# Second mixer: block masks and token scales by ScalarE, the block diagonal issued three steps ahead of its transposes, one tile of sums for a head's chunks

## The chip, the cores and the metric

The kernel runs on one core of one Trainium2 chip. The metric is the device time of one execution in microseconds, the lower the better. TensorE (PE in the profile) multiplies matrices, VectorE (DVE), ScalarE (ACT) and GpSimd (POOL) work elementwise, and SyncE (SP) issues the transfers (DMA). Each engine works through its own list of instructions strictly in the order of the list; an instruction whose input is not there yet holds up everything behind it on that engine.

## The reference, cut to what matters

The whole model is long (two attention layers, then two layers with feed-forward parts, a mixer and cross attention each, for 512 tokens of width 1024). The change touches one mixer alone, the gated delta rule of the second layer, with 8 heads of width 128:

```python
def deltanet_mixer(h, w_in, conv_w, a_log, dt_bias, o_norm, w_out):
    qkv, z, a, b = jnp.split(h @ w_in, ...)
    qkv = jax.nn.silu(causal_dwconv(qkv, conv_w)).astype(jnp.float32)
    q, k, v = jnp.split(qkv, 3, axis=-1)
    q, k, v = l2norm(q.reshape(shp)), l2norm(k.reshape(shp)), v.reshape(shp)
    ...
    o = gated_delta_rule_chunked(q, k, v, g, beta)
    o = rmsnorm(o, o_norm) * jax.nn.silu(z...)
    return o.reshape(B, S, W) @ w_out

def gated_delta_rule_chunked(q, k, v, g, beta):
    ...
    decay = jnp.exp(jnp.where(tril, gcum[..., :, None] - gcum[..., None, :], -jnp.inf))
    kkt = jnp.einsum('bhnid,bhnjd->bhnij', kb, k) * decay
    amat = jnp.eye(C) + jnp.where(strict, kkt, 0.0)
    sol = lax.linalg.triangular_solve(amat, rhs, left_side=True, lower=True, unit_diagonal=True)
    ...
    def step(state, inp):
        v_new = u_i - jnp.einsum('bhcd,bhde->bhce', w_i, state)
        o = (jnp.einsum('bhcd,bhde->bhce', q_i * jnp.exp(g_i)[..., None], state)
             + jnp.einsum('bhij,bhje->bhie', qk_i, v_new))
        state = (state * ... + jnp.einsum('bhcd,bhce->bhde', k_i * ..., v_new))
        return state, o
```

The kernel works with 4 chunks of 128 tokens, so that a head has four 128x128 triangular matrices to invert.

## The kernel before, in words

The mixer (`mixer1`) runs in ten stages, s = 0 to 9. In stage s three generators are woven together: `head(s)` projects and convolves k, q, z and v of head s, makes the decays e and the strictly triangular matrix U; `inverse` inverts the triangular matrices of head s-1; `steps` walks through the four chunks of head s-2 with the running state. Some 41 us pass for each stage. The order on TensorE is the order in which this weave yields; the orders on the other engines are set by a scheduler with priorities and estimated costs, which here can put an instruction far ahead of the place where the code issues it.

The inversion goes in levels. `solve` writes the 16x16 diagonal blocks of U to DRAM, reads them back so that each lies in one partition, and inverts them there on GpSimd with 30 small instructions (L1653 and L1655, T and Y); the result Y goes to DRAM (yd, L1659) and comes back as soC, 128 partitions x 4 x 16 numbers (L1661). `inverse` first spreads soC into the block diagonal X (128x512, four chunks of 128) by one product with a mask of zeros and ones (L1674), transposes it on TensorE (L1683), and then doubles the block size by two levels, with the off-diagonal blocks B, the product of U and another mask (L1692), as input.

Other names: rk, the inverse lengths of the keys, scale e by one product on GpSimd in `key` (L1591). `steps` multiplies the head's output o by the inverse lengths rq, also on GpSimd (L1770), ahead of the transposes of o (L1775). In `steps` the products with the state are po<-state,kT and po<-state,qT (L1732, L1733); R (DVE, L1735) and oq (ACT, L1738) read them; po<-R,X (L1740) gives vn (ACT, L1742); po<-vn,A and po<-vn,kd give o and the new state on DVE. Each chunk takes a new tile of PSUM with the tag "po", of which there is one buffer.

Around them ACT splits weights: wh is the rounded weight (ACT, L114), wl the rest (DVE, L115), from the loaded ws. In the convolution of k, q or v, xp is the padded projection, xc the sum of four shifted copies (one on ACT, L1292, three on DVE, L1296), and kT, qT, vT the result (tanh on ACT, L1536; product on DVE, L1537). kT and vT are transposed on TensorE (L1550) into kd and vb (DVE, L1628, L1629). sq<-kT (ACT, L1578) feeds the lengths (PE, L1580).

Of the kernel before, what the change touches and what calls it, by code (L numbers as in the profile page):

```python
# [8 lines left out]
F32 = mybir.dt.float32  # L9
F32R = mybir.dt.float32r  # L10
I32 = mybir.dt.int32
AF = mybir.ActivationFunctionType
OP = mybir.AluOpType
AX = mybir.AxisListType

P = 128
D = 1024
NCH = 8
S = 512
# [1141 lines left out]
class Block2:  # L1161
# [323 lines left out]
    def decays(self, pool):  # L1485

        net, nc, I = self.net, self.net.nc, self.net.I
        out = {}
        yield from self.proj(I["dn_ab"], out, "p1", 16)
        yield  # L1490
        ab = pool.tile([P, S], F32, name="ab", tag="dnB", bufs=1)[:16, :]
        nc.vector.tensor_tensor(ab, out["ps"], self.rb[:16, :], op=OP.mult)
        pt = net.psum("p3")
        for t in range(4):
            nc.tensor.transpose(pt[:, t * 16:(t + 1) * 16], ab[:, t * P:(t + 1) * P], net.ident[:16, :16])
        t3 = lambda name: pool.tile([P, 4, 8], F32, name=name, tag=f"dc{name}", bufs=1)
        v = pt[:, :64].rearrange("p (t a) -> p t a", a=16)
        dt = net.bcast_row(I["dn_dt_bias_2"][0], 8, "dtb", pool)
        al = net.bcast_row(I["dn_a_log_2"][0], 8, "alog", pool)
        beta, x, gc = t3("beta"), t3("x"), t3("gc")  # L1500
        nc.scalar.activation(beta, v[:, :, 8:16], AF.Tanh, scale=0.5)
        nc.vector.tensor_scalar(beta, beta, 0.5, 0.5, op0=OP.mult, op1=OP.add)
        nc.vector.tensor_tensor(x, v[:, :, 0:8], dt.unsqueeze(1).to_broadcast([P, 4, 8]), op=OP.add)
        sp = self.softplus(x.rearrange("p t h -> p (t h)"), 32, pool)
        nc.scalar.activation(al, al, AF.Exp)
        nc.vector.scalar_tensor_tensor(x, sp.rearrange("p (t h) -> p t h", h=8), -1.0,
                                       al.unsqueeze(1).to_broadcast([P, 4, 8]), op0=OP.mult, op1=OP.mult)
        yield
        pg = net.psum("p3")
        g2 = x.rearrange("p t h -> p (t h)")  # L1510
        nc.tensor.matmul(pg[:, 0:32], net.c["triu"], g2, start=True, stop=True)
        nc.tensor.matmul(pg[:, 32:64], net.c["ones"], g2, start=True, stop=True)
        nc.vector.tensor_copy(gc, pg[:, 0:32].rearrange("p (t h) -> p t h", h=8))
        gl = pg[:, 32:64].rearrange("p (t h) -> p t h", h=8)
        ngc, egc, egl, dk = t3("ngc"), t3("egc"), t3("egl"), t3("dk")
        nc.vector.tensor_scalar(ngc, gc, -1.0, None, op0=OP.mult)
        nc.scalar.activation(egc, gc, AF.Exp)
        nc.scalar.activation(egl, gl, AF.Exp)
        nc.vector.tensor_tensor(dk, gl, gc, op=OP.subtract)
        nc.scalar.activation(dk, dk, AF.Exp)  # L1520
        self.dc = dict(beta=beta, gc=gc, ngc=ngc, egc=egc, egl=egl, dk=dk)
        yield
# [16 lines left out]
    def head(self, h, hd, pool, late):  # L1539

        net, nc, I = self.net, self.net.nc, self.net.I
        cw = self.cw
        q4 = lambda a: a.rearrange("p (t d) -> p t d", d=P)
        bc = lambda a: a.unsqueeze(2).to_broadcast([P, 4, P])
        tl = lambda name, bufs: pool.tile([P, S], F32, name=name, tag=f"dn{name}", bufs=bufs)
# [6 lines left out]
        cols = lambda a: lambda t: a[:, t * P:(t + 1) * P]  # L1552
# [9 lines left out]
        dc, e, U, A = {}, tl("e", 1), tl("U", 2), tl("A", 3)  # L1562
# [21 lines left out]
        def key():  # L1584
            rk = st["k"]
            for n in ("b", "s", "w"):
                st[n] = small("n" + n)
            nc.vector.tensor_tensor(st["b"], rk, dc["beta"], op=OP.mult)
            nc.vector.tensor_tensor(st["s"], rk, dc["dk"], op=OP.mult)
            nc.vector.scalar_tensor_tensor(st["w"], st["b"], -1.0, dc["egc"], op0=OP.mult, op1=OP.mult)  # L1590
            nc.gpsimd.tensor_tensor(out=q4(e), in0=q4(e), in1=bc(rk), op=OP.mult)  # L1591

        def product(m, n):
            ps = net.psum("p3")
# [69 lines left out]
    def inverse(self, hd, pool, wait):  # L1664

        net, nc = self.net, self.net.nc
        mm = nc.tensor.matmul
        q4 = lambda a: a.rearrange("p (t d) -> p t d", d=P)
        tl = lambda name, bufs: pool.tile([P, S], F32, name=name, tag=f"dn{name}", bufs=bufs)
        lev = lambda l: self.lev[:, (l - 4) * P:(l - 3) * P].unsqueeze(1).to_broadcast([P, 4, P])  # L1670
        U = hd["U"]
        hd["X"] = X = tl("X", 2)
        blocks = [P, 4, 8, 16]
        nc.gpsimd.tensor_tensor(out=X.rearrange("p (t m b) -> p t m b", t=4, b=16),  # L1674
                                in0=hd["blocks"].unsqueeze(2).to_broadcast(blocks),
                                in1=self.lev[:, 2 * P:].rearrange("p (m b) -> p m b", b=16).unsqueeze(1).to_broadcast(blocks),
                                op=OP.mult)
        Z = tl("Z", 1)
        for _ in range(wait):
            yield  # L1680
        ps = net.psum("pT")
        for t in range(4):
            nc.tensor.transpose(ps[:, t * P:(t + 1) * P], X[:, t * P:(t + 1) * P], net.ident)  # L1683
        nc.scalar.activation(Z, ps, AF.Copy)
        tiles = [slice(t * P, (t + 1) * P) for t in range(4)]
        for l in range(4, 6):
            n = 1 << l
            half = lambda a, i: a.rearrange("p (m two b) -> p m two b", two=2, b=n)[:, :, i, :]
            dense = lambda a: a.rearrange("p (m b) -> p m b", b=n)
            B, W = tl("B", 1), tl("W", 2)  # L1690
            nc.gpsimd.memset(W, 0.0)
            nc.gpsimd.tensor_tensor(out=q4(B), in0=q4(U), in1=lev(l), op=OP.mult)  # L1692
            yield
            pw = net.psum("pT")
            for t, sl in enumerate(tiles):
                mm(dense(pw[:, t * 64:(t + 1) * 64]), B[:, sl], half(Z[:, sl], 0), start=True, stop=True)
            nc.scalar.activation(half(W, 0), dense(pw[:, :256]), AF.Copy)
            yield
            px = net.psum("p1")
            for t, sl in enumerate(tiles):  # L1700
                mm(dense(px[:, t * 64:(t + 1) * 64]), W[:, sl], half(X[:, sl], 1), start=True, stop=True)
                mm(dense(px[:, 256 + t * 64:256 + (t + 1) * 64]), X[:, sl], half(W[:, sl], 0), start=True, stop=True)
            nc.vector.tensor_tensor(half(X, 1), half(X, 1), dense(px[:, :256]), op=OP.subtract)
            nc.vector.tensor_tensor(half(Z, 0), half(Z, 0), dense(px[:, 256:]), op=OP.subtract)
        yield
        h0, h1 = slice(0, HD), slice(HD, P)
        right = lambda a, t: a[:, t * P + HD:(t + 1) * P]
        pw = net.psum("pT")
        for t in range(4):
            mm(pw[h1, t * HD:(t + 1) * HD], right(U, t)[h0], Z[h0, t * P:t * P + HD], start=True, stop=True)  # L1710
        W = tl("W", 2)
        nc.scalar.activation(W[h1, :256], pw[h1, :256], AF.Copy)
        yield
        px = net.psum("p1")
        for t in range(4):
            mm(px[h0, t * HD:(t + 1) * HD], W[h1, t * HD:(t + 1) * HD], right(X, t)[h1], start=True, stop=True)
        nc.vector.tensor_scalar(q4(X)[h0, :, HD:], px[h0, :256].rearrange("p (t d) -> p t d", d=HD), -1.0, None, op0=OP.mult)

    def steps(self, h, hd, pool):

        net, nc = self.net, self.net.nc
        mm = nc.tensor.matmul
        small = lambda name, bufs=2: pool.tile([P, P], F32, name=name, tag=f"st{name}", bufs=bufs)
        q4 = lambda a: a.rearrange("p (t d) -> p t d", d=P)
        o = pool.tile([P, S], F32, name="o", tag="dno", bufs=2)
        state = None
        for t in range(4):
            sl = slice(t * P, (t + 1) * P)
            ps = net.psum("po")
            R = hd["vb"][:, sl]  # L1730
            if t:
                mm(ps[:, 0:P], hd["kT"][:, sl], state, start=True, stop=True)  # L1732
# [12 lines left out]
            if t < 3:  # L1745
# [7 lines left out]
                state = new  # L1753
# [10 lines left out]
        rq = net.small([P, 4], "orq")  # L1764
# [2 lines left out]
        nc.vector.tensor_tensor(ss, ss, rq, op=OP.mult)  # L1767
        r = net.rsqrt(ss, 4, 1.0 / P, EPS)
        nc.vector.tensor_tensor(rq, r, rq, op=OP.mult)
        nc.gpsimd.tensor_tensor(out=q4(o), in0=q4(o), in1=rq.unsqueeze(2).to_broadcast([P, 4, P]), op=OP.mult)  # L1770

        def finish():
            ps = net.psum("p3")
# [7 lines left out]
    def mixer1(self):  # L1781
        net, nc, I = self.net, self.net.nc, self.net.I
        stats = self.norm("mix_norm_2", 1)
        with net.tc.tile_pool(name="mix1", bufs=2) as pool:
            self.lev = pool.tile([P, 3 * P], F32, name="lev", tag="lev", bufs=1)
            nc.sync.dma_start(self.lev, I["lev"])
            self.cw = pool.tile([P, 96], F32, name="cwh", tag="cwh", bufs=1)
            nc.vector.tensor_scalar(self.cw, net.col["dn_conv_w_2"], 0.5, None, op0=OP.mult)
            hds = [{} for _ in range(8)]
# [373 lines left out]
```

## Time and profile before

| what | value |
|---|---|
| median of 3 runs | 3684.03 us (3679.31 to 3688.05) |
| profiled execution | 3685.61 us, span 3682.5 us |
| PE busy over the span | 3589.7 us, 97% |
| DVE, ACT, POOL busy | 57%, 37%, 19% |
| granted TensorE clock, mean | 0.993 of full speed |

The mixer of the change takes some 400 us of the span, from about 2780 to 3195 us. The profiled execution is one single execution, 1.6 us above the median; all durations below are from it.

### The profile page before, as it was taken

The numbers are of one execution on the slowest core, as the hardware profiler recorded it, in microseconds if no ns is written. First come the engines' busy times: TensorE is split into PE (matmuls) and PEld (weight loads), VectorE is DVE, ScalarE is ACT, GpSimd is POOL, SyncE is SP. The second block draws the span as 40 slices with busy tenths as digits, with TensorE's granted clock in tenths as the row PEclk, the third lists the DMA queues.
The fourth block names the chain that finished last, engine by engine and source line by source line (L and its number), as shares of the span: only waits on it lengthen the run. The fifth ranks groups of instructions, "written<-read, shape, count | busy, mean of one in ns | idle before, by whom it ended". The sixth has DMA issues, their size and how long they took to land.

```text
span 3682.5 us, 51253 instructions
## 1 busy us (share of the span) xinstructions
PE 3589.7 (97%) x19626; PEld 2992.9 (81%) x19626; DVE 2096.6 (57%) x4095; ACT 1380.4 (37%) x2413; POOL 715.7 (19%) x889
## 2 busy tenths in 40 slices
PE   8999999999999999999999999999999999999998
PEld 6888778888877778888778888888888887788887
DVE  6655765875566553335666433443347887664335
ACT  4334543244345332224644322322243333443223
POOL 1123330003233010101420100110013444101001
PEclk9999999999999999999999999999999999999999
DMA  8322115533212533333122333333333212323333
GB/s 278 101 73 63 49 54 192 160 123 97 83 62 68 194 103 96 96 92 107 54 98 69 98 97 98 97 92 103 97 98 112 57 56 74 116 78 92 102 96 106
DMA packets 137012, 366.68 MB, mean 100 GB/s; under 512 B 30144, under 2 KB 43712, under 8 KB 136256
## 3 DMA queue, kind: packets, MB, share of 16 engines
q1 hardware_dynamic: 136768, 363.42, 31.7%
q8 instruction: 154, 2.52, 0.3%
q14 instruction: 90, 0.74, 0.1%
HBM read 332.82 MB, written 20.84 MB: 96 GB/s over the span
## 4 chain that ended last, share of the span: by engine, by line
PE 85%; DVE 7%; DMA 3%; ACT 2%; issue 1%; POOL 1%; SPq 0%; DVEq 0%; ACTq 0%; POOLq 0%
PE p L131 14%; PE p L133 14%; PE p L132 14%; PE pS L131 7%; PE pS L132 6%; PE pS L133 6%; PE po L562 2%; PE po L131 2%; PE po L133 2%; PE po L132 2%; DVE wl L115 2%; PE pT L132 2%; PE pT L131 2%; PE pT L133 2%; PE pS L536 1%
## 5 line engine op out<-in xcount | busy, mean ns | idle before, releaser
L114 ACT ACTIVATE wh<-ws 128x1024 fp32r<-128x1024 f32 (+4 forms) x561 | 563.3, 1006 | 1395.4 <-PE p L132 673.3
L115 DVE TENSOR_TENSOR wl<-ws,wh 128x1024 fp32r<-128x1024 f32 (+4 forms) x561 | 659.2, 1176 | 224.4 <-ACT wh L114 222.4
L131 PE MATMUL p<-nh,wh 128*128 128x512 f32 x1084 | 430.1, 397 | 4.5 <-ACT nh L1179 2.0
L133 PE MATMUL p<-nh,wl 128*128 128x512 f32 x1084 | 424.0, 391 | 4.0 <-DVE wl L115 4.0
L132 PE MATMUL p<-nl,wh 128*128 128x512 f32 x1084 | 423.9, 391 | 1.9 <-DVE nl L115 1.9
L1246 POOL TENSOR_TENSOR g<-g,rb 128x512 f32<-128x512 f32 x88 | 150.2, 1709 | 1138.3 <-ACT g L1245 1138.3
L131 PE MATMUL pS<-nh,wh 128*128 128x512 f32 x620 | 255.1, 411 | 1.0 <-DVE xr L1229 1.0
L133 PEld LDWEIGHTS p<-nh,wl 128*128 128x128 f32 x1084 | 203.3, 188 | 49.4 <-DVE wl L115 5.5
L133 PE MATMUL pS<-nh,wl 128*128 128x512 f32 x620 | 243.4, 393 | 0.0
L132 PE MATMUL pS<-nl,wh 128*128 128x512 f32 x620 | 242.7, 391 | 0.0
L131 PEld LDWEIGHTS p<-nh,wh 128*128 128x128 f32 x1084 | 203.5, 188 | 47.0 <-ACT nh L1179 2.4
L132 PEld LDWEIGHTS p<-nl,wh 128*128 128x128 f32 x1084 | 203.7, 188 | 42.1 <-DVE nl L115 2.2
L1244 DVE TENSOR_TENSOR g<-p,rb 128x512 f32<-128x512 f32 x88 | 60.4, 691 | 226.5 <-PE p L133 213.4
L131 PE MATMUL p<-hxh,wh 128*128 128x512 f32 (+1 forms) x480 | 187.3, 390 | 0.8 <-DVE wT L545 0.8
L132 PE MATMUL p<-hl,wh 128*128 128x512 f32 (+1 forms) x488 | 179.8, 369 | 0.0
L133 PE MATMUL p<-hh,wl 128*128 128x512 f32 (+1 forms) x488 | 179.4, 368 | 0.0
L131 PE MATMUL p<-hh,wh 128*128 128x512 f32 (+1 forms) x488 | 179.3, 368 | 0.0
L133 PE MATMUL p<-hxh,wl 128*128 128x512 f32 (+1 forms) x480 | 173.5, 361 | 0.0
L132 PE MATMUL p<-hxl,wh 128*128 128x512 f32 (+1 forms) x480 | 172.9, 360 | 0.0
L1188 POOL TENSOR_TENSOR acc<-acc,sq 128x512 f32<-128x512 f32 x48 | 73.9, 1539 | 483.2 <-ACT sq L1187 482.8
L552 POOL TENSOR_SCALAR p<-p,rinv 128x768 f32<-128x768 f32 (+2 forms) x128 | 104.4, 816 | 254.5 <-DVE rinv L551 138.4
L1259 DVE SCALAR_TENSOR_TENSOR xr<-p,xr 128x512 f32<-128x512 f32 (+1 forms) x68 | 42.6, 627 | 169.4 <-PE p L133 169.2
(605 smaller groups left out, 8779.8 us busy)
## 6 DMA issues: line engine op xcount, KB each, us to landing
ws<-in_ffn_w_in_dram SPq DMA_DIRECT2D x176, 512.0 KB
ws<-in_ffn_w_out_dram SPq DMA_DIRECT2D x64, 512.0 KB
ws<-in_w_in_tok_dram SPq DMA_DIRECT2D x52, 512.0 KB
aw<-in_w_ada_dram SPq DMA_DIRECT2D x32, 512.0 KB
ws<-in_ffn_w_out_dram SPq DMA_DIRECT2D x40, 384.0 KB
ws<-in_w_out_dram SPq DMA_DIRECT2D x24, 512.0 KB
ws<-in_dn_qkv_dram SPq DMA_DIRECT2D x24, 512.0 KB
wh<-in_w_ada_dram SPq DMA_DIRECT2D x16, 512.0 KB
```

The costliest lines, as they stand in the source:

```text
L114: self.last_hi = self.nc.scalar.activation(hi, src, AF.Copy)
L115: (eng or self.nc.vector).tensor_tensor(out=lo, in0=src, in1=hi.bitcast(F32), op=OP.subtract)
L131: mm(pt, sh, mh, start=first and i == 0, stop=False)
L132: mm(pt, sh, ml, start=False, stop=False)
L133: mm(pt, sl, mh, start=False, stop=last and i == n - 1)
L536: mm(ps, q, kA[:, k0:k1], start=True, stop=False)
L552: nc.gpsimd.tensor_scalar(p, p, r, 0.5, op0=OP.mult, op1=OP.mult)
L562: self.net.nc.tensor.matmul(ps[h:h + HD, :], v, w, start=i < 2, stop=i >= len(parts) - 2)
L1188: (nc.vector if c == 7 else nc.gpsimd).tensor_tensor(out=acc, in0=acc, in1=sq, op=OP.add)
L1244: nc.vector.tensor_tensor(t, pg, self.rb, op=OP.mult)
L1246: nc.gpsimd.tensor_tensor(out=t, in0=t, in1=self.rb, op=OP.mult)
L1259: nc.vector.scalar_tensor_tensor(x, ps, 0.5, x, op0=OP.mult, op1=OP.add)
```

## The change

In `key` and `steps` the scaling of e by rk and of o by rq goes from one GpSimd product of 128x512 to four ACT copies of 128x128 each, with the scale from a column. In `inverse` the mask products go to ACT as well: X is written by eight copies of 128 x (4x16), each with a column of zeros and ones as scale, and they are issued in the code three steps of the weave ahead of X's transposes rather than at the generator's start; the masked off-diagonal blocks B by four and by two copies, into two B tiles that are zeroed once. The columns are cut from the mask by three small copies at the start. In `steps`, the four chunks of a head share one PSUM tile.

```diff
@@ key
-            nc.gpsimd.tensor_tensor(out=q4(e), in0=q4(e), in1=bc(rk), op=OP.mult)
+            for t in range(4):
+                nc.scalar.activation(cols(e)(t), cols(e)(t), AF.Copy, scale=rk[:, t:t + 1])
@@ inverse
-        blocks = [P, 4, 8, 16]
-        nc.gpsimd.tensor_tensor(out=X.rearrange("p (t m b) -> p t m b", t=4, b=16),
-                                in0=hd["blocks"].unsqueeze(2).to_broadcast(blocks),
-                                in1=self.lev[:, 2 * P:].rearrange("p (m b) -> p m b", b=16).unsqueeze(1).to_broadcast(blocks),
-                                op=OP.mult)
         Z = tl("Z", 1)
-        for _ in range(wait):
+        for i in range(wait):
+            if i == wait - 3:
+                for m in range(8):
+                    nc.scalar.activation(q4(X)[:, :, 16 * m:16 * m + 16], hd["blocks"], AF.Copy, scale=self.rows[2][:, m:m + 1])
             yield
...
-            B, W = tl("B", 1), tl("W", 2)
+            B, W = self.B[l - 4], tl("W", 2)
             nc.gpsimd.memset(W, 0.0)
-            nc.gpsimd.tensor_tensor(out=q4(B), in0=q4(U), in1=lev(l), op=OP.mult)
+            for m in range(64 // n):
+                at = slice((2 * m + 1) * n, (2 * m + 2) * n)
+                nc.scalar.activation(q4(B)[:, :, at], q4(U)[:, :, at], AF.Copy, scale=self.rows[l - 4][:, m:m + 1])
@@ steps
-        state = None
+        state, ps = None, net.psum("po")
         for t in range(4):
             sl = slice(t * P, (t + 1) * P)
-            ps = net.psum("po")
...
-        nc.gpsimd.tensor_tensor(out=q4(o), in0=q4(o), in1=rq.unsqueeze(2).to_broadcast([P, 4, P]), op=OP.mult)
+        for t in range(4):
+            nc.scalar.activation(o[:, t * P:(t + 1) * P], o[:, t * P:(t + 1) * P], AF.Copy, scale=rq[:, t:t + 1])
@@ mixer1
-            self.lev = pool.tile([P, 3 * P], F32, name="lev", tag="lev", bufs=1)
-            nc.sync.dma_start(self.lev, I["lev"])
+
+            self.B = [pool.tile([P, S], F32, name="B", tag=f"dnB{l}", bufs=1) for l in range(2)]
+            for b in self.B:
+                nc.gpsimd.memset(b, 0.0)
+            lev = pool.tile([P, S], F32, name="lev", tag="dnsq", bufs=1)[:, :3 * P]
+            nc.sync.dma_start(lev, I["lev"])
+            self.rows = []
+            for i, (a, n, w) in enumerate(((16, 4, 32), (32, 2, 64), (0, 8, 16))):
+                r = pool.tile([P, n], F32, name="rows", tag=f"rows{i}", bufs=1)
+                v = lev[:, i * P:(i + 1) * P].rearrange("p (m b) -> p m b", b=w)
+                nc.vector.tensor_copy(r, v[:, :, a])
+                self.rows.append(r)
```

One more line gives the tile ab of `decays` another tag. The order on TensorE is the same as before but for the line numbers.

On ACT, in the stage that inverts the first head (head 0), this stood behind the vT of that head; X was not on ACT:

```order
L1536 ACTIVATE vT<-xc 128x512
L114 ACTIVATE wh<-ws 128x1024
L1292 ACTIVATE xc<-xp,cwh 128x512
L114 ACTIVATE wh<-ws 128x1024
L1573 ACTIVATE e<-e,ngc 128x128 x4
L1536 ACTIVATE kT<-xc 128x512
L114 ACTIVATE wh<-ws 128x1024
L1292 ACTIVATE xc<-xp,cwh 128x512
L1578 ACTIVATE sq<-kT 128x512
```

and now this stands there:

```order
L1536 ACTIVATE vT<-xc 128x512
L114 ACTIVATE wh<-ws 128x1024
L1292 ACTIVATE xc<-xp,cwh 128x512
L114 ACTIVATE wh<-ws 128x1024
L1677 ACTIVATE X<-soC,rows 128x4x16 x8
L1573 ACTIVATE e<-e,ngc 128x128 x4
L1536 ACTIVATE kT<-xc 128x512
L114 ACTIVATE wh<-ws 128x1024
L1292 ACTIVATE xc<-xp,cwh 128x512
L1578 ACTIVATE sq<-kT 128x512
```

The eight X, which wait for soC, stand ahead of the next head's e, kT and sq, and of a weight.

In each of the stages that invert heads 2 to 6, ACT had this order from vT on:

```order
L1536 ACTIVATE vT<-xc 128x512
L1738 ACTIVATE oq<-po,egc 128x128
L114 ACTIVATE wh<-ws 128x1024
L1742 ACTIVATE vn<-po 128x128
L1292 ACTIVATE xc<-xp,cwh 128x512
L1573 ACTIVATE e<-e,ngc 128x128 x4
L1536 ACTIVATE kT<-xc 128x512
```

and has this one now (head 1 has X ahead of oq, else the same):

```order
L1536 ACTIVATE vT<-xc 128x512
L1737 ACTIVATE oq<-po,egc 128x128
L1677 ACTIVATE X<-soC,rows 128x4x16 x8
L114 ACTIVATE wh<-ws 128x1024
L1741 ACTIVATE vn<-po 128x128
L1292 ACTIVATE xc<-xp,cwh 128x512
L1573 ACTIVATE e<-e,ngc 128x128 x4
L1536 ACTIVATE kT<-xc 128x512
```

X stands ahead of a weight's wh, of vn and of the next xc. At the same place DVE had

```order
L1296 SCALAR_TENSOR_TENSOR xc<-xp,cwh,xc 128x512 x2
L1735 SCALAR_TENSOR_TENSOR R<-po,nw,vb 128x128
L1537 SCALAR_TENSOR_TENSOR vT<-vT,xc 128x512
L1628 TENSOR_TENSOR kd<-p_26318,ns 128x512
L1629 TENSOR_TENSOR vb<-p_26324,beta 128x512
L1289 TENSOR_TENSOR xp<-pS,rb 128x512
```

and has

```order
L1296 SCALAR_TENSOR_TENSOR xc<-xp,cwh,xc 128x512 x2
L1734 SCALAR_TENSOR_TENSOR R<-po,nw,vb 128x128
L1629 TENSOR_TENSOR kd<-p_26353,ns 128x512
L1537 SCALAR_TENSOR_TENSOR vT<-vT,xc 128x512
L1630 TENSOR_TENSOR vb<-p_26359,beta 128x512
L1289 TENSOR_TENSOR xp<-pS,rb 128x512
```

kd and vT have changed places, in five heads. In the stage of head 7 ACT had

```order
L332 ACTIVATE m_28532<-ws,cols 128x256 x2
L1536 ACTIVATE vT<-xc 128x512
L332 ACTIVATE m_28533<-ws,cols 128x256 x2
L1738 ACTIVATE oq<-po,egc 128x128
L1742 ACTIVATE vn<-po 128x128
L114 ACTIVATE wh<-ws 128x1024
L114 ACTIVATE nh<-y 128x512
```

and has

```order
L1536 ACTIVATE vT<-xc 128x512
L1770 ACTIVATE o<-o,orq 128x128 x4
L1677 ACTIVATE X<-soC,rows 128x4x16 x7
L332 ACTIVATE m_28630<-ws,cols 128x256 x2
L1677 ACTIVATE X<-soC,rows 128x4x16
L1737 ACTIVATE oq<-po,egc 128x128
L1741 ACTIVATE vn<-po 128x128
L114 ACTIVATE nh<-y 128x512
L114 ACTIVATE wh<-ws 128x1024
```

Here X, and a pair of m (memory tiles of the cross attention), stand ahead of oq.

## Rows read from the trace of the kernel before

**Rows 1.** Busy time by stretch: PE, PEld, DVE, ACT, POOL (instructions); clock, DMA share, GB/s.

```profile
2780.00:3195.00 415.00, 393.14 (x2344) 333.52 (x2343) 326.63 (x726) 160.62 (x298) 159.56 (x320) 0.99 0.26 77
```

**Rows 2.** PE's waits, 2700 to 3250 us: us in total, times, longest.

```profile
PE po L1732 <- DVE o L1755: 5.4, 6, 1.0
PE p L1550 <- DVE vT L1537: 2.6, 5, 0.5
```

**Rows 3.** Timeline of PE, one stage: start, length, in brackets the idle time before.

```profile
2931.76 0.66 PE L1550 MATMUL p<-c_ident,vT 128*128 128x128 f32 x4 [0.53 <-DVE vT L1537]
...
2939.84 0.49 PE L1732 MATMUL po<-state,kT 128*128 128x128 f32 x2 [1.04 <-DVE o L1755]
```

**Rows 4.** Timeline of ACT in the same stage.

```profile
2933.61 1.06 ACT L114 ACTIVATE wh<-ws 128x1024 fp32r<-128x1024 f32 x1 [2.38 <-PE pS L132]
...
2934.73 0.71 ACT L1292 ACTIVATE xc<-xp,cwh 128x512 f32<-128x512 f32 x1
2938.77 1.28 ACT L1573 ACTIVATE e<-e,ngc 128x128 f32<-128x128 f32 x4 [3.32 <-DVE e L1570]
```

**Rows 5.** Timeline of DVE in the same stage.

```profile
2931.01 0.69 DVE L1537 SCALAR_TENSOR_TENSOR vT<-vT,xc 128x512 f32<-128x512 f32 x1 [0.44 <-ACT vT L1536]
2931.62 0.68 DVE L1628 TENSOR_TENSOR kd<-p,ns 128x512 f32<-128x512 f32 x1
...
2935.17 1.22 DVE L115 TENSOR_TENSOR wl<-ws,wh 128x1024 fp32r<-128x1024 f32 x1
2936.30 1.77 DVE L1296 SCALAR_TENSOR_TENSOR xc<-xp,cwh,xc 128x512 f32<-128x512 f32 x1
...
2938.60 0.73 DVE L1296 SCALAR_TENSOR_TENSOR xc<-xp,cwh,xc 128x512 f32<-128x512 f32 x1
...
2939.51 0.28 DVE L1755 TENSOR_TENSOR o<-po,oq 128x128 f32<-128x128 f32 x1
```

**Rows 6.** Timeline of POOL in the same stage.

```profile
2925.40 1.03 POOL L1770 TENSOR_TENSOR o<-o,orq 128x512 f32<-128x512 f32 x1
...
2936.02 1.50 POOL L1674 TENSOR_TENSOR X<-soC,lev 128x512 f32<-128x512 f32 x1 [3.92 <-DMA soC<-yd]
```

**Rows 7.** Line L1573 by form: ns of one, min/median/max.

```profile
L1573 ACT ACTIVATE e<-e,ngc x32: 384/386/404, 2787.3 to 3062.0; 128x128 f32<-128x128 f32 x32
```

**Rows 8.** Timelines of ACT, POOL and PE, stage that inverts head 0.

```profile
2816.55 0.61 ACT L1578 ACTIVATE sq<-kT 128x512 f32<-128x512 f32 x1
...
2820.43 1.28 POOL L1674 TENSOR_TENSOR X<-soC,lev 128x512 f32<-128x512 f32 x1 [4.69 <-DMA soC<-yd]
...
2817.22 1.19 PE L1580 MATMUL p<-c_ones,sq 128*128 128x1 f32 x8 [1.46 <-ACT sq L1578]
```

**Rows 9.** Timelines of POOL and PE, stage that inverts head 1.

```profile
2853.43 1.66 POOL L1674 TENSOR_TENSOR X<-soC,lev 128x512 f32<-128x512 f32 x1 [3.98 <-DMA soC<-yd]
...
2851.67 0.38 PE L1740 MATMUL po<-R,X 128*128 128x128 f32 x2
```

**Rows 10.** Timelines of POOL and PE, stage that inverts head 7.

```profile
3101.64 1.89 POOL L1674 TENSOR_TENSOR X<-soC,lev 128x512 f32<-128x512 f32 x1 [2.98 <-DMA soC<-yd]
...
3097.77 0.49 PE L1740 MATMUL po<-R,X 128*128 128x128 f32 x2 [1.09 <-ACT oq L1738]
3098.71 0.66 PE L1775 MATMUL p<-c_ident,o 128*128 128x128 f32 x4 [0.45 <-POOL o L1770]
...
3101.73 0.51 PE L131 MATMUL p<-nh,wh 128*128 128x512 f32 x1 [0.97 <-ACT nh L114]
3104.13 0.50 PE L132 MATMUL p<-nl,wh 128*128 128x512 f32 x1 [1.90 <-DVE nl L115]
```

**Rows 11.** Busy time behind two of PE's waits, clock in the third column from the end.

```profile
2818.00:2821.50 3.50, 3.50 (x14) 3.11 (x14) 3.34 (x9) 0.63 (x1) 1.07 (x1) 0.51 0.38 62
1910.60:1914.00 3.40, 3.40 (x15) 2.83 (x16) 3.40 (x5) 2.47 (x4) 0.00 (x0) 1.00 0.39 95
```

**Rows 12.** Timeline of PE, the wait ahead of the second of these stretches.

```profile
1910.58 0.50 PE L131 MATMUL p<-nh,wh 128*128 128x512 f32 x1 [1.42 <-DVE xr L1229]
```

More of the change, by code (lines that the diff above doesn't have):

```diff
@@ L1490, in decays @@
         yield
-        ab = pool.tile([P, S], F32, name="ab", tag="dnB", bufs=1)[:16, :]
+        ab = pool.tile([P, S], F32, name="ab", tag="dnW", bufs=2)[:16, :]
         nc.vector.tensor_tensor(ab, out["ps"], self.rb[:16, :], op=OP.mult)
@@ L1669, in inverse @@
         tl = lambda name, bufs: pool.tile([P, S], F32, name=name, tag=f"dn{name}", bufs=bufs)
-        lev = lambda l: self.lev[:, (l - 4) * P:(l - 3) * P].unsqueeze(1).to_broadcast([P, 4, P])
         U = hd["U"]
         hd["X"] = X = tl("X", 2)
-        blocks = [P, 4, 8, 16]
-        nc.gpsimd.tensor_tensor(out=X.rearrange("p (t m b) -> p t m b", t=4, b=16),
-                                in0=hd["blocks"].unsqueeze(2).to_broadcast(blocks),
-                                in1=self.lev[:, 2 * P:].rearrange("p (m b) -> p m b", b=16).unsqueeze(1).to_broadcast(blocks),
-                                op=OP.mult)
         Z = tl("Z", 1)
-        for _ in range(wait):
+        for i in range(wait):
+            if i == wait - 3:
+                for m in range(8):
+                    nc.scalar.activation(q4(X)[:, :, 16 * m:16 * m + 16], hd["blocks"], AF.Copy, scale=self.rows[2][:, m:m + 1])
             yield
```

## The prediction

> **What bounds the kernel now.** I first read the busy shares: over the 415 us of the changed mixer PE works 393.1 us, DVE 326.6, ACT 160.6 and POOL 159.6, at a granted clock of 0.99 [rows 1]. PE bounds the kernel; all it can win here is its idle time, 415.0 - 393.1 = 21.9 us, 0.6% of the whole. Next I read whom PE waits for. The two regular waits are that of L1732 for the o of DVE, six times and 5.4 us in total, and that of L1550 for vT, five times and 2.6 us [rows 2]. In a regular stage that is 0.53 us for vT and 1.04 us for o [rows 3]. Some larger waits stand at the first and the last head [rows 8, 10]. GpSimd itself stops PE in one place only, 0.45 us for o at L1775 [rows 10].
>
> POOL matters indirectly. Its X starts at 2936.02 and lasts 1.50 us, and the DVE instruction beside it, an xc, takes 1.77 us instead of the 0.73 us of the same instruction a little later [rows 5, 6]. This 1.04 us sits in the list of DVE ahead of state and o, for which PE then waits 1.04 us [rows 3, 5]. So the change does aim at something real.
>
> X is also the one moved product that waits long for its input: 3.92, 4.69, 3.98 and 2.98 us in four stages, always for soC to come back from DRAM [rows 6, 8, 9, 10]. On POOL nothing urgent stands behind it. The question is what stands behind it on ACT.
>
> **Price of the ACT instructions.** A copy of 128x128 with a column as operand takes 0.386 us [rows 7], four in a row 1.28 us [rows 4], so a further one costs (1.28 - 0.386)/3 = 0.30 us. A copy of 128x512 takes 0.71 us [rows 4], so an element costs (0.713 - 0.386)/384 = 0.85 ns. No row shows a copy of 64 elements; from these I estimate 0.33 us alone and 0.24 us for each further one. X is then 0.33 + 7 x 0.24 = 2.0 us, B 1.06 and 0.68, each of e and o 1.28 us, in sum 6.3 us a head. Bounds for X: 8 x 64 x 0.85 ns = 0.4 us if only the elements counted, 8 x 0.33 = 2.6 us without any overlap; I keep 2.0, next to the four copies of e.
>
> ACT works 160.6 of 415 us, so that 8 x 6.3 = 50 us more fit by load: 51%. B and the scales e and o read inputs that are there when their turn comes, apart from 0.2 us (1.28 against the 1.04 of a POOL product as in [rows 6]) in front of U and of the transposes of o, which have slack. I price them at nothing; were the cover gone at each head, it would be 8 x 0.5 = 4 us. The Trainium skill speaks against the move: "ScalarE: Activation LUTs", section "Rules for kernel authors", wants multiplications on VectorE and not on ScalarE. The trace agrees on the price of one: 0.68 us for kd on DVE and 1.28 us for the same 512 columns on ACT [rows 4, 5]. By that rule alone all of the 50 us would count against the change; by the busy share of ACT none would, and the sum uses the share. The single PSUM tile of a head takes no wait away: PE's next product with the state still waits for o on DVE, as before. I price that at nothing too, and the three small copies at the start likewise.
>
> What costs is the order.
>
> **Heads 2 to 6, kd ahead of vT.** Until now DVE made vT at 2931.01 (0.69) and then kd at 2931.62 (0.68), and PE transposed vT at 2931.76 after 0.53 us of waiting [rows 3, 5]. Now kd comes first, as soon as PE has transposed kT (which it had by 2931.23, 0.53 us before 2931.76). Then kd runs from about 2931.3 to 2931.9, vT is ready near 2932.6 instead of 2931.76, and PE waits about 1.4 us instead of 0.53: **+0.85** a head.
>
> **Heads 2 to 6, X on ACT.** ACT is free from 2933.61 - 2.38 = 2931.23 on [rows 4] and then stands at X until soC lands. Before, that was at 2936.02 [rows 6]. The solve on POOL, which leads to soC, now has the 1.03 us of o (2925.40) out of its middle [rows 6] and starts a little earlier; I bound the gain by 1.0 and 1.8 us and take 1.6. So soC lands near 2934.4, X is done at 2936.4, and the wh of 2933.61 starts 2.8 us late. Behind it wl (2935.17) cannot start before wh has ended, at 2937.4: 2.25 us late [rows 4, 5]. Behind wl on DVE stand xc, e, state and o. The clash with POOL gives back 1.04, so o is 1.2 us late. PE itself comes 0.85 us later to L1732. Its wait there grows from 1.04 to about 1.4 us: **+0.35**, with bounds of -0.1 (all but a trifle of X hidden) and +0.85. Together 1.2 a head, **+6 us** for five heads.
>
> **Head 0.** Here X stands ahead of e, kT, wh, xc and sq. ACT comes there long before soC and stops. It goes on when soC lands, at 2820.43 as before, since this solve has no o in it [rows 8]; X takes until 2822.4. Then come four e (1.28), kT (0.63), wh (1.06), xc (0.71) and sq (0.61), some 4.0 us with their overlaps. PE's L1580, now at 2817.22 behind sq, moves to about 2826.4: **+9.2 us**. With an X of 0.4 or 2.6 us it is +7.6 to +9.8. If soC came 2 us sooner it would be +7.
>
> **Head 1.** X stands ahead of oq, and oq is read first among what chunk 1 needs: PE's L1740 runs at 2851.67 without a wait [rows 9]. soC lands between 2852.2 (one POOL product of 1.2 us less in the solve) and 2853.4 [rows 9], X and oq add 2.35, so L1740 waits until 2854.5 to 2855.8: 2.9 to 4.1 us. The later wait of 1.0 for o is hidden by it. I take **+2.5**.
>
> **Head 7.** Seven X, a pair of m and the last X stand ahead of oq. soC at 3101.64, or 0.4 us sooner without o [rows 10]; X, m (0.9) and oq end near 3104.4, while L1740 ran at 3097.77: +6.7. From what followed I take off 0.45 for o, 0.97 for nh, and 1.4 of the 1.90 for nl, which a clash with X had stretched [rows 10]: **+3.9**, bounds 2 and 6.
>
> **Clock.** Behind the wait of 1.46 us at 2817.22 the granted clock was 0.51, half speed, that is 1.2 instead of 2.4 GHz, for 3.5 us, which costs about 1.7 us [rows 8, 11]. Behind a wait of 1.42 us elsewhere it stayed 1.00 [rows 11, 12]. So the new waits of 1.4 us in five stages may cost anything from 0 to 10 x 1.7 = 17 us. I charge one fall, for the wait of about 3 us at head 1: **+1.6**. At heads 0 and 7 the clock has fallen before as well.
>
> **Sum:** 6 + 9.2 + 2.5 + 3.9 + 1.6 = 23.2 us on the 3685.6 us of the profiled execution, 3708.8. That execution lies 1.6 us above the median of 3684.0, so a median should be near **3707**, +0.6%. A measurement of this kernel can tell about 0.2%, 7.4 us, from no change.
>
> **Rivals.**
> *Faster: the clash goes and X costs nothing.* If soC lands before ACT arrives at X, or if what stands behind X has more slack than I see, the regular waits for o shrink from 1.04 to nothing: 6 less 5.4 us [rows 2], and POOL's o at L1775 another 0.5. Some 3678. The port shared by VectorE and GpSimd in "Advanced Engine Details and Errata" (section "VectorE Performance Modes") of the Trainium skill is the rule behind it, and the rows of xc agree with it. Against it stands that X waited 3 to 4.7 us in every stage shown. It decides if soC lands over 3 us sooner. Chance 0.05.
> *No difference: gain and loss cancel.* Head 0 costs less (a weight is loaded far ahead and e, kT are not needed when I say), heads 2 to 6 win 1 us each by the clash and lose it by kd: 3680 to 3691. Chance 0.10.
> *Worse: the clock.* Waits of 1.4 us twice in each of five stages bring it down at most of them: 3707 + 8 to 17 = 3715 to 3724. For it speaks that 1.4 lies next to 1.46; against it the 1.42 us with a full clock. Chance 0.20.
> *The forecast:* 3695 to 3715, chance 0.65.
>
> **How the numbers follow.** The range 3689 to 3721 holds the forecast, most of the clock's case and the edge of the cancelling one. Slower by over 0.2% (above 3691.4) are forecast and clock: 0.85; the same 0.10; faster (under 3676.7) takes most of the first rival, 0.05.
>
> **What would show it.** Right: on ACT an idle time of some 10 us ahead of X in the stage of head 0, released by soC, and one of about 3 us in each later stage; PE's longest wait in the mixer at L1580 behind sq, some 10 us; waits for oq of 3 us and 7 us at heads 1 and 7; waits for vT of 1.4 us in five stages; every xc of DVE at 0.73 to 0.8. Wrong: L1580 starting within 3 us of its old place, waits for vT as before, or an idle ACT without anyone waiting for it. Should PE's idle time in the mixer not grow beyond 30 us, the prediction has failed in its main step.

## The result and the profile after

The changed kernel takes 3708.98 us (median of 4 runs, 3705.34 to 3714.0), the kernel before 3683.37 (4 runs): a ratio of 1.0071, 95% interval 1.0054 to 1.0089. That is 25.6 us slower; 3707 was forecast, within 3689 to 3721.

The profiled execution of the change took 3714.0 us with a span of 3712.2, 29.7 more than before. First the busy time of a stretch of 442 us that holds its mixer, to be read against the 415 us of [rows 1] (the ends of both are cut by hand): PE, PEld, DVE, ACT, POOL, then clock, DMA share and GB/s.

```profile
2780.00:3222.00 442.00, 398.71 (x2360) 337.88 (x2359) 302.62 (x738) 208.35 (x475) 106.00 (x281) 0.97 0.25 74
```

ACT has 48 us more work and POOL 54 less, as counted, and DVE is busy 24 us less, since POOL stretches fewer of its instructions. PE works 6 us more (parts at the lower clock) and idles 43 us instead of 22. PE's waits in the view of waits, 2700 to 3280 us (us in total, times, longest), name the places:

```profile
PE po L1739 <- ACT oq L1737: 11.2, 4, 7.1
PE p L1580 <- ACT sq L1578: 10.2, 1, 10.2
PE p L1550 <- DVE vT L1537: 6.9, 5, 1.4
PE po L1731 <- DVE o L1754: 6.6, 5, 1.4
...
PE po L1743 <- ACT vn L1741: 0.7, 3, 0.3
```

Against [rows 2], vT went from 2.6 to 6.9 and o from 5.4 to 6.6; the wait behind sq grew from 1.46 us [rows 8] to 10.15, and that for oq to 11.2.

Where did it start? The timeline of ACT in the stage that inverts head 0:

```profile
2812.53 1.04 ACT L114 ACTIVATE wh<-ws 128x1024 fp32r<-128x1024 f32 x1
2823.42 2.02 ACT L1677 ACTIVATE X<-soC,rows 128x64 f32<-128x64 f32 x8 [9.85 <-DMA soC<-yd]
2825.34 1.26 ACT L1573 ACTIVATE e<-e,ngc 128x128 f32<-128x128 f32 x4
2826.51 0.61 ACT L1536 ACTIVATE kT<-xc 128x512 f32<-128x512 f32 x1
2827.03 1.04 ACT L114 ACTIVATE wh<-ws 128x1024 fp32r<-128x1024 f32 x1
2827.97 0.71 ACT L1292 ACTIVATE xc<-xp,cwh 128x512 f32<-128x512 f32 x1
2828.58 0.61 ACT L1578 ACTIVATE sq<-kT 128x512 f32<-128x512 f32 x1
```

ACT stands idle for 9.85 us in front of X, and then does X and the five kinds of work behind it without a gap. PE gets its sq 12 us later in the span than before [rows 8] (3.4 us of this it brings along from ahead of the mixer), as its own timeline shows (with the wait at head 1, a regular stage, and head 7 below it):

```profile
2829.25 1.87 PE L1580 MATMUL p<-c_ones,sq 128*128 128x1 f32 x8 [10.15 <-ACT sq L1578]
...
2868.06 0.57 PE L1739 MATMUL po<-R,X 128*128 128x128 f32 x2 [3.42 <-ACT oq L1737]
...
2951.14 0.66 PE L1550 MATMUL p<-c_ident,vT 128*128 128x128 f32 x4 [1.38 <-DVE vT L1537]
2956.52 0.49 PE L1743 MATMUL po<-vn,A 128*128 128x128 f32 x2 [0.17 <-ACT vn L1741]
2960.01 0.49 PE L1731 MATMUL po<-state,kT 128*128 128x128 f32 x2 [1.38 <-DVE o L1754]
...
3129.10 0.80 PE L1739 MATMUL po<-R,X 128*128 128x128 f32 x2 [7.15 <-ACT oq L1737]
```

The regular stage on ACT, to be read against [rows 4]:

```profile
2953.34 2.02 ACT L1677 ACTIVATE X<-soC,rows 128x64 f32<-128x64 f32 x8 [3.67 <-DMA soC<-yd]
2955.27 1.04 ACT L114 ACTIVATE wh<-ws 128x1024 fp32r<-128x1024 f32 x1
2956.22 0.25 ACT L1741 ACTIVATE vn<-po 128x128 f32<-128x128 f32 x1
```

and on DVE, against [rows 5]:

```profile
2949.79 0.69 DVE L1629 TENSOR_TENSOR kd<-p,ns 128x512 f32<-128x512 f32 x1 [0.78 <-PE p L1550]
2950.40 0.68 DVE L1537 SCALAR_TENSOR_TENSOR vT<-vT,xc 128x512 f32<-128x512 f32 x1
...
2956.34 1.23 DVE L115 TENSOR_TENSOR wl<-ws,wh 128x1024 fp32r<-128x1024 f32 x1 [1.72 <-ACT wh L114]
2957.48 0.75 DVE L1296 SCALAR_TENSOR_TENSOR xc<-xp,cwh,xc 128x512 f32<-128x512 f32 x1
```

X occupies ACT for 2.02 us (2.0 was estimated), wh and wl come behind it, and the xc that took 1.77 us takes 0.75: the clash with POOL is gone, but the wait for X, with wh and wl behind it, costs more than that gives back.

The granted clock behind three of the waits (third column from the end; 1.00 is 2.4 GHz, 0.50 is 1.2 GHz, a value between them a mixture), in windows of the same run:

```profile
2868.00:2872.50 4.50, 4.44 (x16) 3.63 (x17) 2.39 (x3) 1.72 (x4) 0.00 (x0) 0.62 0.22 74
2829.20:2833.00 3.80, 3.75 (x14) 3.46 (x15) 3.25 (x10) 0.63 (x1) 0.10 (x1) 0.50 0.44 138
2917.10:2923.00 5.90, 5.84 (x33) 5.06 (x33) 4.55 (x10) 3.48 (x7) 0.10 (x1) 1.00 0.10 38
```

It was low behind the waits of 3.4 and 10 us, and stayed full behind those of 1.38, here the first for o; from 2835 to 3124 us the clock was low nowhere but behind the 3.4.

### The profile page after: what moved, and what is told of

The parts are those of the page before. It is cut to its first block, busy times and chain, and to the rows that moved or that the text cites. A ratio compares the mean times of both kernels' runs of the same rounds, so it can differ in the third digit from the quotient of the medians.

```text
span 3712.2 us, 51393 instructions
## 1 busy us (share of the span) xinstructions
PE 3594.9 (97%) x19626; PEld 2998.4 (81%) x19626; DVE 2070.4 (56%) x4098; ACT 1426.7 (38%) x2589; POOL 661.9 (18%) x851
## 4 chain that ended last, share of the span: by engine, by line
PE 84%; DVE 6%; DMA 4%; ACT 2%; POOL 2%; issue 2%; SPq 0%; DVEq 0%; POOLq 0%; ACTq 0%
PE p L131 15%; PE p L133 14%; PE p L132 14%; PE pS L131 6%; PE pS L132 6%; PE pS L133 6%; PE po L562 2%; PE po L133 2%; PE po L132 2%; PE po L131 2%; PE pT L132 2%; PE pT L133 2%; PE pT L131 2%; DVE wl L115 1%; PE pS L536 1%
## 5 line engine op out<-in xcount | busy, mean ns | idle before, releaser
L132 PEld LDWEIGHTS p<-nl,wh 128*128 128x128 f32 x1084 | 203.8, 188 | 40.1 <-DVE nl L1180 0.4
L133 PEld LDWEIGHTS pS<-nh,wl 128*128 128x128 f32 x620 | 116.9, 189 | 25.4
```

Source lines behind the costliest of these rows:

```text
L132: mm(pt, sh, ml, start=False, stop=False)
L133: mm(pt, sl, mh, start=False, stop=last and i == n - 1)
```

## The experiments

Theory A, that of the prediction: the amount of work on ACT is free, the place of X in ACT's order costs, since X waits for soC and everything behind it waits too. Theory B: ACT's added work costs by its amount. Below, the length of a regular stage is the distance of the same matmul (L1550 for vT, or po<-state,kT) in two successive stages of heads 2 to 5; before it is 41.2 us, in the change 42.85.

**X back on GpSimd, the rest of the change kept** (`e1`). The product of before is put back in front of Z, the eight copies go. (The lines that load its mask into a tile of its own are left out here.)

```diff
+        nc.gpsimd.tensor_tensor(out=X.rearrange("p (t m b) -> p t m b", t=4, b=16),
+                                in0=hd["blocks"].unsqueeze(2).to_broadcast(blocks),
+                                in1=self.levx..., op=OP.mult)
-                for m in range(8):
-                    nc.scalar.activation(q4(X)[:, :, 16 * m:16 * m + 16], hd["blocks"], AF.Copy, scale=self.rows[2][:, m:m + 1])
```

> The whole change, but X stays one GpSimd product. Theory A (the order on ACT: X, waiting for soC, holds up what is behind it): the waits at L1580 (10 us), at oq of head 1 (3.4) and of head 7 (7.1) fall back to 1.5, 0 and 1; kd still stands ahead of vT, so vT waits 1.4 us, and o, which is bound by the clash of X with an xc, some 0.2 instead of 1.0: time within 4 us of before, 3680 to 3688. Theory B (ACT's added work costs by its amount): X is 2.0 of the 6.3 us a head, so two thirds of the +25 us stay, 3697 to 3703.

Measured: 3683.22 against 3683.92 us, ratio 0.9998 (0.9988 to 1.0007); a stage takes 41.05 us. The whole loss hangs on X; e, B and o on ACT, and the single tile, cost together nothing that these runs can tell. PE's waits in this run:

```profile
PE p L1550 <- DVE vT L1537: 6.9, 5, 1.4
...
PE p L1580 <- ACT sq L1578: 1.5, 1, 1.5
PE po L1733 <- DVE o L1756: 1.0, 1, 1.0
```

The wait for vT is as in the change, yet no time is lost: the five waits for o are gone in exchange. X starts sooner now, 4.15 instead of 5.39 us behind PE's transposes of kT, since o no longer stands in the middle of the solve on POOL:

```profile
2933.10 1.30 POOL L1674 TENSOR_TENSOR X<-soC,levx 128x512 f32<-128x512 f32 x1 [3.87 <-DMA soC<-yd]
```

```profile
2933.01 0.69 DVE L1289 TENSOR_TENSOR xp<-pS,rb 128x512 f32<-128x512 f32 x1 [0.69 <-PE pS L133]
2933.67 0.75 DVE L1779 SCALAR_TENSOR_TENSOR y<-p,cols,z 128x512 f32<-128x512 f32 x1
```

These are POOL's row and DVE's rows at the same moment. X lies beside xp and y, which read PSUM, and stretches neither.

**X alone on ACT, all else as before** (`e2`): the mirror image of the first. (The lines that make the columns are left out here.)

```diff
-        nc.gpsimd.tensor_tensor(out=X..., op=OP.mult)
+                for m in range(8):
+                    nc.scalar.activation(q4(X)[:, :, 16 * m:16 * m + 16], hd["blocks"], AF.Copy, scale=self.rows[2][:, m:m + 1])
```

> The kernel before, with X alone moved to ACT. Theory A: head 0 +9 us; head 1 +4; in heads 2 to 6 soC lands later than in the change, since GpSimd keeps o inside the solve, so the wait for o grows from 1.0 to about 3 to 4 us, +2.5 a head; head 7 +5: in sum +30 us, 3713 and so slower than the whole change. Theory B (amount of work): a third of +25, some 3692.

Measured: 3719.43 us, ratio 1.0099 (1.0086 to 1.0112), some 36 us slower with a third of the added ACT work: slower than the whole change. Theory B is out. A stage takes 44.2 to 45.4 us, where 41.2 + 2.5 was forecast, and the place was another one than I expected. It isn't o that PE waits for:

```profile
PE p L1580 <- ACT sq L1578: 12.8, 6, 9.4
PE po L1742 <- ACT vn L1740: 11.5, 5, 2.8
PE po L1738 <- ACT oq L1736: 10.8, 4, 7.2
```

vn, which stands on ACT directly behind X and wh, comes 2 to 3 us late, and o is then waited for no longer, but for once 0.7 us. Part of the surplus is the clock: behind four of the five waits for vn it was at half speed for most of the next 3.5 us (0.52 to 0.62 over that stretch), behind the fifth, of 2.23 us, it stayed full.

**The whole change with X later on ACT** (`e3`). In the code, X is put behind an ACT instruction at which soC has landed:

```diff
+                self.behind = self.t0 if wait == 16 else self.nh if self.last else self.xc0
+                with net.tc.issue_after(self.behind.ins):
```

(t0 is the tanh of qT, xc0 the ACT part of the last convolution, nh that of y. The eight copies stand in the body; the lines that keep t0, xc0 and nh are left out here.)

> The whole change, with the eight copies X behind an ACT instruction that comes later (head 0: behind the next head's qT, heads 1 to 6: behind xc, ahead of e; head 7: behind nh), where ACT was idle and soC has landed. Theory A: no wait of over 2 us at L1580 or at oq is left; the wait for o is 0 to 0.2, as the clash is gone, that for vT 1.4: 3677 to 3684. Theory B: ACT does just as much, the time stays near 3709.

Measured: 3677.81 against 3683.92 us, ratio 0.9987 (0.9978 to 0.9995); a stage 41.05 us. ACT does the same work as in the change and the 25 us are gone. X now fills a gap of ACT without a wait:

```profile
2924.79 0.71 ACT L1292 ACTIVATE xc<-xp,cwh 128x512 f32<-128x512 f32 x1
2925.40 2.01 ACT L1679 ACTIVATE X<-soC,rows 128x64 f32<-128x64 f32 x8
2927.74 1.28 ACT L1573 ACTIVATE e<-e,ngc 128x128 f32<-128x128 f32 x4 [0.33 <-DVE e L1570]
```

**The same, with vT ahead of kd** (`e5`): kd is put behind vT on DVE.

```diff
+            with net.tc.issue_after(hd["vT_"].ins):
+                nc.vector.tensor_tensor(q4(kd), q4(pk), bc(st["s"]), op=OP.mult)
```

> As the run with X behind a later instruction, and vT ahead of kd on DVE again in heads 2 to 6. Theory A: the waits for vT fall to 0.5 us, those for o stay below 0.3, five heads win 0.85 us against that run: 3672 to 3680, less than before by 4 to 10 us. Theory B: near 3709 still. If the order of kd and vT meant nothing, it equals that run.

Measured: 3672.36 against 3683.92 us, ratio 0.9970 (0.9960 to 0.9979): 11 us faster than before. A stage takes 40.1 us, 0.95 less than in the run above; the waits for vT are 0.42 to 0.44 us and o is not waited for.

**The whole change with vT ahead of kd** (`e4`): the same lines, with X where the change has it.

> The whole change, with vT ahead of kd on DVE again in heads 2 to 6 and X where the change has it. Theory A: within a stage o hangs on soC by way of X, wh and wl, not on vT; the waits for vT fall from 1.4 to 0.4, those for o grow from 1.4 to about 2.3, and the time stays within 2 us of the change, 3707 to 3711. Theory C (the two terms of the prediction, kd ahead of vT and X ahead of wh, add up): 5 x 0.85 = 4 us less, some 3704.5.

Measured: 3707.6 us, ratio 1.0065 (1.0053 to 1.0077). A stage takes 42.8 us, just as in the change. Of PE's waits

```profile
PE po L1733 <- DVE o L1756: 6.6, 5, 1.4
PE po L1745 <- ACT vn L1743: 5.1, 5, 1.1
...
PE p L1550 <- DVE vT L1537: 2.2, 5, 0.5
```

vT is 4.7 us down and vn 4.4 us up; o did not move. The order of kd and vT costs nothing while X holds up vn behind it. I had the growth at o instead of at vn; the sum was right.

**X on GpSimd with vT ahead of kd** (`e7`), the edits of the first and the fourth run together.

> X on GpSimd, the rest of the change, and vT ahead of kd. In the run with X on GpSimd the X lay beside xp and y, which read PSUM and were not stretched; with vT first these come 0.95 us sooner and X falls beside wl, which reads SBUF alone. If GpSimd stretches such a DVE instruction, wl takes about 2.2 instead of 1.2 us, o waits about 1 us again, and the time is 3681 to 3685. If it does not, five stages win 0.95 us: some 3678.

Measured: 3680.52 against 3683.03 us, ratio 0.9998 (0.9989 to 1.0007); a stage 41.05 us. The 0.95 us won at vT came back at o (5.2 us, six times, where `e1` waited once, 1.0 us), and the cause stands in two rows, POOL's and DVE's:

```profile
2932.08 1.29 POOL L1676 TENSOR_TENSOR X<-soC,levx 128x512 f32<-128x512 f32 x1 [3.97 <-DMA soC<-yd]
```

```profile
2932.26 2.19 DVE L115 TENSOR_TENSOR wl<-ws,wh 128x1024 fp32r<-128x1024 f32 x1
```

wl, 1.23 us in the change where no X is beside it, takes 2.19 beside X.

**X of head 0 alone moved** (`e8`), the rest as in the change.

```diff
+                with net.tc.issue_after(self.t0.ins) if wait == 16 else ExitStack():
```

> The whole change, with X of head 0 alone moved behind the next head's qT. Theory A: the wait of 10.2 us at L1580 falls to 1.5, all other waits stay: 9 us less than the change, some 3700. Theory B (amount of work): no difference from the change.

Measured: 3693.92 us, ratio 1.0035 (1.0023 to 1.0047) where the change has 1.0071. The wait at L1580 is back at 1.46 us, those for vT, o and at head 7 (7.2) are as in the change, that for oq at head 1 is 2.4 instead of 3.4, which I had not expected. The two ratios differ by 13 us, with intervals of 4 and 6 us, where I had forecast 9. The profiles say what the rest is. From the first transposes of gc to a matmul at the end of head 7's stage, the change and then this run:

```profile
2788.17:3147.30 359.13, 322.66 (x1974) 276.51 (x1975) 248.99 (x622) 168.25 (x403) 96.56 (x274) 0.97 0.22 64
2777.42:3122.84 345.42, 318.83 (x1974) 273.08 (x1975) 248.72 (x622) 168.11 (x403) 96.08 (x274) 0.99 0.23 66
```

The stretch is 13.7 us shorter: PE idles 9.9 us less, and takes 3.8 us less for the same 1974 matmuls. That part is the clock: in the change it was low for 4.9 us behind L1580's wait and for 3.4 us behind that for oq at head 1, some 4 us lost at half speed (an estimate); here it stayed full behind both (1.00 over the next 3.5 us each).

**X late on ACT, all else as before** (`e9`): the edits of `e2` and `e3`.

> The kernel before, with X alone on ACT, but late (behind qT, xc or nh), vT ahead of kd as before. Theory A: no POOL product lies beside the xc any more, the wait for o of 1.04 us goes at heads 1 to 6, that for vT stays 0.5: 40.2 us a stage instead of 41.2, 3676 to 3679. If the gain of the late X came from e, B and o on ACT instead, it stays at 3684.

Measured: 3672.04 against 3683.03 us, ratio 0.9971 (0.9962 to 0.9980). A stage takes 40.0 to 40.2 us and no wait for o is listed. It is as fast as `e5`, somewhat better than expected: the gain needs X off GpSimd and in a good place, and neither e, B, o nor the tile. The place need not be perfect: X still waited 0.6 to 1.1 us for soC in the stages of heads 2 to 6.

**One tile of sums alone** (`e6`):

```diff
-        state = None
+        state, ps = None, net.psum("po")
         for t in range(4):
             sl = slice(t * P, (t + 1) * P)
-            ps = net.psum("po")
```

> The kernel before with one PSUM tile for the four chunks of a head, and nothing else of the change. All theories but one: PE waits at L1732 for o as before, 1.04 us in five stages, 41.2 us a stage, the time within 4 us of before. If the shared tile took a wait away or added one, the stage length would move by 0.2 us or more.

Measured: 3683.63 against 3679.76 us, ratio 1.0009 (1.0000 to 1.0018); a stage takes 41.15 us and the wait for o is 1.02 to 1.05 us in the first four of its six cases, as before. No difference that this kernel's runs can tell.

## Why the prediction was right, step by step

Growth is read off from the start of the same matmul (po<-state,kT) in both traces, from one stage to the next, and at the front from the first transposes of gc (2784.7 before, 2788.2 in the change).

| step | forecast | measured |
|---|---|---|
| head 0 | +9.2 | +9.4 |
| head 1, with a fall of the clock | +2.5 + 1.6 | +4.1 |
| heads 2 to 6 | +6 | +8.6 (1.6 to 2.0 each) |
| head 7 | +3.9 | +2.7 |
| sum in the mixer | +23.2 | +24.7 |

The sum is as near as it is because a term that was too small (heads 2 to 6) and one that was too large (head 7) took some of each other away; that much is luck.

**Head 0** held as worked out: soC, then X, e, kT, wh, xc, sq. Of the 9.4 us, 8.8 are PE's idle time; 0.6 are PE's work at the lower clock, which lasted longer than before and which I had put at nothing here. `e8` takes this wait away, and with it 1 us of that for oq and the falls of the clock at heads 0 and 1.

**Head 1** too: the wait for oq grew to 3.42 us, the 1.0 us for o went, and PE ran at half speed for 3.4 us behind it: 2.4 us more idle time and 1.7 us more for the same work.

**Heads 2 to 6**: the mechanism was right, the term was 0.4 to 0.8 us a head short. I had taken soC to land 1.6 us sooner without o in the solve; it landed 1.2 us sooner, as X starts 4.18 us behind PE's transposes of kT in the change (2953.34, in the stage shown) and 5.39 us before (2936.02). That is 0.4 us of it, and within the bounds of 1.0 and 1.8. Also, part of the delay showed at vn (up to 0.25 us), which I had left out. And the split into +0.85 for kd and +0.35 for X was not a split of causes: vT first wins 0.95 us a stage where X is late (from `e3` to `e5`), and nothing where X holds up vn (from the change to `e4`). In the change, the chain soC, X, wh, vn and wl sets the stage, and the wait for vT lies within it.

**Head 7**: L1739 waited 7.15 us; of the four waits of [rows 10], 4.41 us in sum, all were gone. 7.15 - 4.41 = 2.7; I had taken off only 2.8 for what followed instead of 3.3, and put L1739 0.6 too late.

**Clock**: one fall more was charged and one came. The waits of 1.38 us left it at full speed in every stage of the profiled execution, so the rival of the clock did not come true. The length of a wait alone does not decide this, so it was no sure thing. Behind the 1.46 us at L1580 the clock fell in the kernel before [rows 11], but stayed full behind the same wait in all seven runs that have it (`e1`, `e3` and `e5` to `e9`); in `e1`:

```profile
2818.00:2821.50 3.50, 3.50 (x20) 3.04 (x21) 3.36 (x9) 0.63 (x1) 1.37 (x3) 1.00 0.50 96
```

The other way round, it stayed full behind 2.36 us in `e8` and fell behind 2.46 us at the same place in `e4`.

The first rival (faster) is what `e5` and `e9` are: it needed X in a place where soC has landed or nearly so, not soC in time for the place that X had.

The profiled executions differ by 5 us more than the mixer: 3.4 ahead of it and 1.6 behind. The 3.4 are there well ahead of the mixer: the same product u on DVE (L1248) starts at 2703.3 before and at 2706.8 in the change. The first transposes of gc lie at 2774.6 to 2784.8 in the other runs here. I take these 5 us for the spread of executions (the profiled one is the slowest of the change's four, 5 us above their median).

The price of ACT's work was rightly put at nothing. The rule of the Trainium skill ("ScalarE: Activation LUTs", section "Rules for kernel authors") that multiplications belong on VectorE was no guide to the time here: with 48 us more on ACT, `e3` and `e5` are faster than the kernel before.

## What to carry to other kernels

Before moving an instruction to another engine, read how long it waits for its input and what stands behind it there; on an engine in strict order a late input holds up everyone behind it, however idle the engine is on average. A copy that waits belongs behind the work that is ready, which may be later in the order than a scheduler's estimate of the input puts it. And where several waits lie on one chain, removing one shows the next: price the stage, not the wait.

## What the runs showed of the hardware that had not been expected

A GpSimd product of 128x512 stretches the DVE instruction that starts while it runs by about 1 us where that reads SBUF alone (xc from 0.73 to 1.77 in [rows 5], wl from 1.23 to 2.19 in `e7`), but not one that reads PSUM: xp and y took 0.69 and 0.75 us beside X in `e1`. Where the DVE instruction was first, GpSimd takes longer instead. At head 7 of `e7` wl started 0.06 us ahead of X and kept its length, while X took 2.28 us instead of 1.29 (the X of 1.50 us in [rows 6] also starts beside a wl under way):

```profile
3097.46 1.23 DVE L115 TENSOR_TENSOR wl<-ws,wh 128x1024 fp32r<-128x1024 f32 x1
3097.52 2.28 POOL L1676 TENSOR_TENSOR X<-soC,levx 128x512 f32<-128x512 f32 x1 [4.00 <-DMA soC<-yd]
```

The Trainium skill ("Advanced Engine Details and Errata", section "VectorE Performance Modes") says that GpSimd and those DVE instructions that use the second SBUF port block each other; the stretched rows agree, in both directions, and the rows of xp and y show which were spared here. Which port an instruction uses no row shows. So the same product costs 1 us a stage or nothing, by the moment at which it falls.
